# HGRN head outputs turned by VectorE in squares of 32 and put in place by their stores, instead of TensorE products with the identity

## The chip, the cores and the metric

The kernel runs on one core of one Trainium2 chip, as one program with one launch. The metric is the device time in microseconds (us) of that launch. A comparison of two versions goes by medians of several runs on the same chip.

## The reference, cut to what matters

A layer takes x, 1024 tokens of 1024 features, normalises it, projects it with `w_in` to some 5,600 columns and runs three causal mixers on them: a Mamba-2 SSD with 16 heads, an HGRN2 recurrence with 4 heads of 128, and an S5 with 32 groups. Their outputs, 2048 features in all, are multiplied with `w_out`, normalised again and added to x. Everything is float32. The change touches the HGRN part only:

```python
def hgrn2_mixer(q, f_raw, i_in, g, lb, norm_w):
    ...
    def step(state, inp):
        qc, kc, vc, lfc = inp
        cum = jnp.cumsum(lfc, axis=2)
        decay = jnp.exp(jnp.where(mask, cum[:, :, :, None, :] - cum[:, :, None, :, :], -jnp.inf))
        attn = jnp.einsum("bhlk,bhsk,bhlsk->bhls", qc, kc, decay)
        o = (jnp.einsum("bhls,bhsv->bhlv", attn, vc)
             + jnp.einsum("bhlk,bhkv->bhlv", qc * jnp.exp(cum), state))
        ...
    _, o = lax.scan(step, state0, (to_chunks(q), to_chunks(k), to_chunks(i_in), to_chunks(log_f)))
    o = o.transpose(1, 0, 3, 2, 4).reshape(bsz, seqlen, HGRN_WIDTH)
    return grouped_rms_norm(o, norm_w, HGRN_HEADS) * jax.nn.silu(g)
```

The normalisation runs over the 128 values of one head at one token. In the kernel it is done while tokens lie on the partitions (one token, one partition), since the sum then runs along a row. The product with `w_out`, much later, wants features on the partitions. So each head's normalised output, 1024 tokens by 128 values, has to be turned: eight squares of 128 by 128.

## The kernel before, in words

**Products.** TensorE computes nearly everything that is a matrix product. The large projections (`project`, `side_by_side`, `values`) and the output product split each float32 operand into a high and a low part of a rounded format (fp32r) and add three products (`mm3`); these are the rows `p<-r,v`, `p<-y,r`, `p<-s,v` and `c<-s,s` of the profile. A projection of one block of 128 columns is 48 such products of 128x512. The small products of the three mixers stay plain float32: rows with `m`, `h` or `ident` behind the arrow, which write the PSUM tiles `c` (four of them, given out in turn). Some use the whole array (128 wide), some only squares of it: the HGRN decay products are 32 wide and 64 wide, the last products of an SSD chunk 64 wide.

**An HGRN head** (`hgrn_core`, four times). Seven levels of a binary decay tree: at each level TensorE multiplies k with q' (32 small products, or 16, or 8), and VectorE multiplies k and q' by that level's decay. VectorE must wait until TensorE has read k, and TensorE's next level needs the new k, so a head is a chain of round trips between the two; projections of other columns stand between the levels on TensorE. Then k is turned by eight TensorE transposes into `kt`, seven products with `kt` give the states, VectorE chains them, and 15 products give the head's output `pss` in two PSUM tiles. ScalarE squares it, VectorE sums, a reciprocal root and a few tiny operations make the scale `ms`, and two VectorE multiplications write the normalised output to the tile `ot`. At the end, eight transposes (`T.transpose`, a product with the identity `ident`) write `ot` turned into two PSUM tiles, two ScalarE copies move these to the tile `o_`, and one store on SP's queue puts `o_` into the scratch tensor `hm_d` in DRAM, 512 bytes per piece. `out_gate` reads `hm_d` in the last part of the kernel.

**The order of the work.** It isn't that of the source. `trunk` records every instruction of the five engines, `depends` works out what each needs, and `improve` plays a list scheduler (`arrange`) forwards and backwards over them with a cost for each kind of instruction; `force` then fixes the resulting order on every engine and on the DMA queues. Each engine works strictly in that order. `BYTES` and `TRIP` are the planner's transfer rate and landing time, `KEEP` is how strongly it avoids changing TensorE's kind of product (or ScalarE's function table), `ROOMS` are margins it adds to durations and hand-offs, and `SHUFFLES` lists the planner's rounds: seed of a random shake of the ranks, its size, number of passes, and which row of `ROOMS` is in force. So an edit anywhere can move instructions everywhere.

SP issues nearly all stores and loads in its fixed order; the weight loads stand in ScalarE's queue.

Of the kernel before, what the change touches and what calls it, by code (L numbers as in the profile page):

```python
# [16 lines left out]
P = 128  # L17
# [3 lines left out]
NCH = L // P  # L21
# [155 lines left out]
    return steps + [x for *_, x in turn]  # L177


SWITCH, LOAD, BYTES, TRIP, LANES = 165.0, 1283.0, 370.0, 2000.0, 8  # L180

STEP, KEEP = 130.0, {"PE": 3000.0, "Activation": 3000.0}

ROOMS = (
    {"PE": (1.0, 200.0), "DVE": (1.06, 100.0), "Activation": (1.05, 100.0), "Pool": (1.1, 100.0)},
# [1 line left out]
    {"PE": (1.0, 300.0), "DVE": (1.06, 200.0), "Activation": (1.05, 200.0), "Pool": (1.05, 200.0)},  # L187
)

SHUFFLES = ((70, 1000.0, 4, 2), (148, 100.0, 0, 2), (165, 30.0, 1, 2), (285, 100.0, 0, 2), (331, 30.0, 0, 2), (355, 30.0, 0, 2), (376, 100.0, 0, 2), (442, 30.0, 0, 2), (529, 100.0, 0, 2), (630, 30.0, 0, 2), (726, 100.0, 0, 2))  # L190


def arrange(steps, rank, back=False):
# [92 lines left out]
def improve(steps, rank):  # L286

    plain = [(s.len, s.post) for s in steps if s.eng]
    for seed, by, passes, room in SHUFFLES:
        for s, (n, post) in zip((s for s in steps if s.eng), plain):  # L290
# [20 lines left out]
def trunk(ctx: ExitStack, tc: tile.TileContext, a: dict, out: bass.AP, dbg=None):  # L311
    nc = tc.nc
    book, bundles = [], []
    V, A, G, T, S = [Engine(e, book) for e in (nc.vector, nc.scalar, nc.gpsimd, nc.tensor, nc.sync)]
# [33 lines left out]
    def get(kind):  # L348
        return pools[kind].pop(0)

    def free(*ts_):
        for t in ts_:
            kind, t0 = home[t.tensor.name]
            pools[kind].append(t0)
# [11 lines left out]
    def ring(kind):  # L366
        t = banks[kind].pop(0)
        banks[kind].append(t)
        return t

    def slot():
        return get("m")
# [4 lines left out]
    def bank():  # L377
        return ring("c")
# [4 lines left out]
    def mul(eng, o, x, y):  # L383
        eng.tensor_tensor(out=o, in0=x, in1=y, op=ALU.mult)
# [23 lines left out]
    def mm3(o, lh, ll, rh, rl, start, stop):  # L408
        T.matmul(o, lh, rh, start=start, stop=False)
        T.matmul(o, lh, rl, start=False, stop=False)  # L410
        T.matmul(o, ll, rh, start=False, stop=stop)

    def total(o, x, h, l, eng=None):

        split(x, h, l, eng or V)
        T.matmul(o, onesr, h, start=True, stop=False)
        T.matmul(o, onesr, l, start=False, stop=True)

    def load_const(name, shape, dt=F32, src=None):
        t = cst.tile(shape, dt, tag=name, name=name)  # L420
        S.dma_start(t, a[name] if src is None else src)
        return t
# [12 lines left out]
    def c3(x, c=4):  # L435
        return x.rearrange("p (c l) -> p c l", c=c)
# [5 lines left out]
    HS = [slice(0, HALF), slice(HALF, L)]  # L442
# [33 lines left out]
    def side_by_side(ms, ps, each=lambda k: None):  # L476

        ws = [weights(a["w_in"][m]) for m in ms]
        for k in range(KD):
            each(k)  # L480
            for w, p in zip(ws, ps):
                wh, wl = [c3(t)[:, k % 4] for t in w[k // 4]]
                for n in range(2):
                    mm3(p[n], wh, wl, hh[k][:, HS[n]], hl[k][:, HS[n]], k == 0, k == KD - 1)
            if k % 4 == 3:
                for w in ws:
                    free(*w[k // 4])
# [5 lines left out]
    def begin(ms):  # L493
# [22 lines left out]
        for k in range(KD):  # L516
            h, l = get("r"), get("r")
            hf, i = k // 4, k % 4
            for t in range(2):
                if i == 0:  # L520
                    ws[t].append((get("v"), get("v")))
                if k < 2:
                    cols = (head, rest)[k]
                    split(wr[t][:, cols], *[x[:, cols] for x in ws[t][0]], V)
                elif i == 0:
                    split(wr[t][:, HS[hf]], *ws[t][hf], V)
                if t == 0:
                    for s in HS if k == 0 else [slice(0, L)]:
                        act(h[:, s], xs[k][:, s], AF.Copy, scale=prew[:, k:k + 1])
                        stt(l[:, s], xs[k][:, s], prew[:, k:k + 1], h[:, s].bitcast(F32), ALU.mult, ALU.subtract)  # L530
                wh, wl = ws[t][hf]
                for n in range(2):
                    mm3(ps[t][1][n], c3(wh)[:, i], c3(wl)[:, i], h[:, HS[n]], l[:, HS[n]], k == 0, k == KD - 1)
            if i == 3:
                for w in ws:
                    free(*w[hf])
            hh.append(h)
            hl.append(l)
            sq = acc if k == 0 else get("x")
            act(sq, xs[k], AF.Square)  # L540
            if k > 0:
                add(V, acc, acc, sq)
                free(sq)
# [35 lines left out]
    with tc.high_priority(offset=2 * PRI):  # L579
        first, rsb = begin((F0, Q0))  # L580

        ps = [[bank(), bank()], [bank(), bank()]]
        side_by_side((U0, U0 + 1), ps)
        for b in range(2):
            t = get("x")
# [12 lines left out]
    ident = load_const("ident", [P, P])  # L598
# [28 lines left out]
    def scratch(name, shape):  # L627
        return dr.tile(shape, F32, name=name)
# [3 lines left out]
    hm_d = scratch("hm_d", [NCH, P, 4, P])  # L632
# [115 lines left out]
    def hgrn_core(hd, f, k, q, v):  # L748
        qp, at, tots = slot(), slot(), slot()
# [13 lines left out]
        def product(qq, h=None, t=1):  # L763

            ps = bank()
            n = 32 if h is None else 16
            for c in range(NCH):
                for j in range(4):
                    s = slice(c * P + 32 * j, c * P + 32 * j + 32)
                    o, x = ps[32 * j:32 * j + 32, c * n:(c + 1) * n], qq[:, s]  # L770
                    if h is not None:
                        x = x.rearrange("p (n t h) -> p n t h", t=2, h=h)[:, :, t, :]
                        o = o.rearrange("p (n h) -> p n h", h=h)
                    T.matmul(o, k[:, s], x, start=True, stop=True)
            return ps[:, 0:NCH * n].rearrange("p (c l) -> p c l", c=NCH)
# [20 lines left out]
        for h in (1, 2, 4, 8, 16, 32, 64):  # L796
            n = L // (2 * h)
            tv = tot.rearrange("p (n t) -> p n t", t=2)
            if h == 2:

                A.copy(q.rearrange("p (n h t) -> p n h t", h=2, t=2)[:, :, :, 0], halves(qp, h)[:, :, 1, :])
                ps = product(q)
# [3 lines left out]
            elif h == 32:  # L806
                ps = bank()
# [5 lines left out]
                for j in range(4):  # L813
                    b, t = j // 2, j % 2
                    A.copy(at.rearrange("p (c t l) -> p c t l", t=2, l=P)[64 * b:64 * b + 32, :, t, 64 * b + 32:64 * b + 64],
                           ps[32 * j:32 * j + 32, 0:4 * 32].rearrange("p (c l) -> p c l", l=32))
            elif h == 64:

                ps = bank()
# [23 lines left out]
        for hf in range(2):  # L843
            ps = bank()
# [5 lines left out]
        for hf in range(2):  # L850
            ps = bank()
            for c in range(4):
                i = hf * 4 + c
# [4 lines left out]
            for c in range(4):  # L858
                i = hf * 4 + c
# [10 lines left out]
        ot, o_ = slot(), slot()  # L870
# [3 lines left out]
        for hf in range(2):  # L874
            ps = bank()
            pss.append(ps)
            for c in range(4):
                i = hf * 4 + c
# [14 lines left out]
        stt(ms, zs, 1.5, ys, ALU.add, ALU.mult)  # L893
        for hf in range(2):
            mul(V, c3(ot[:, HS[hf]]), c3(pss[hf]), ms[:, hf * 4:hf * 4 + 4].unsqueeze(2).to_broadcast([P, 4, P]))
        for hf in range(2):
            ps = bank()
            for c in range(4):
                i = hf * 4 + c
                T.transpose(ps[:, c * P:(c + 1) * P], ot[:, i * P:(i + 1) * P], ident)  # L900
            A.copy(o_[:, HS[hf]], ps)
        free(ot)
        if dbg is not None:
            S.dma_start(dbg["ho"][hd], o_)
        S.dma_start(hm_d[:, :, hd, :].rearrange("c p l -> p c l"), c3(o_, NCH))
        free(o_)


# [650 lines left out]
    for _ in range(2):  # L1559
        t = get("x")  # L1560
# [116 lines left out]
```

## Time and profile before

| | |
|---|---|
| median of 3 runs | 858.48 us (857.78 to 858.52) |
| profiled execution | 858.45 us |
| its span, first to last instruction | 856.7 us |
| TensorE busy (PE) | 848.2 us, 99% of the span |
| VectorE (DVE) | 563.9 us, 66% |
| ScalarE (ACT) | 399.6 us, 47% |
| GpSimd (POOL) | 249.6 us, 29% |
| granted TensorE clock | 0.999 |

The span is what the trace shows; 1.75 us of the profiled execution lie around it. In the profile every operation that a helper records stands at line 39, so groups are told apart by the names of their tiles: `c<-ident,m` is a transpose of an `m` tile into a PSUM tile `c`, `m<-c` a copy back, `hrs` the small tile of the normalisation. A plain float32 product appears as two records, a transpose or an fp32r product as one. The duration of a TensorE record contains its way through the array and overlaps the next; what an instruction takes from the engine is the distance from its start to the next start, which the timeline shows.

### The profile page before, as it was taken

The page shows a single profiled execution, that of the slowest core. Times are in us where ns is not written, and L with a number is a line of the kernel's source. Part 1 is how long each engine was busy: PE and PEld are TensorE (multiplying, and loading weights), DVE is VectorE, ACT ScalarE, POOL GpSimd, SP SyncE. Part 2 cuts the span into 40 slices and gives each one's busy share as a digit, 9 for nine tenths or more (in the row PEclk, how much of TensorE's full clock was granted, in tenths as well). Part 3 has the DMA queues.
Part 4 walks back from the last instruction along what each step waited for, and adds up shares of the span by engine and source line. Part 5 has one row for each costly group of instructions (what it writes and reads, how often), then busy time and mean ns, then how long its engine had stood idle before and what let it go on. Part 6 is the DMA issues. An engine that isn't in the chain of part 4 may idle for free.

```text
span 856.7 us, 14902 instructions
## 1 busy us (share of the span) xinstructions
PE 848.2 (99%) x5873; PEld 707.5 (83%) x5873; DVE 563.9 (66%) x1003; ACT 399.6 (47%) x637; POOL 249.6 (29%) x224
## 2 busy tenths in 40 slices
PE   8999999999999999999999999999999999999997
PEld 6888988789887888788888887788887888888886
DVE  6978399996479686785163756677646878544521
ACT  8556145455234535244237887851736833322210
POOL 0565032433143225232321234353214232111000
PEclk9999999999999999999999999999999999999999
DMA  7323012337233432448646798756957745344110
GB/s 258 112 79 120 3 51 75 101 97 217 52 95 93 122 102 63 95 117 228 181 119 219 220 269 255 240 167 205 350 153 241 239 168 197 111 136 135 62 50 25
DMA packets 92038, 124.67 MB, mean 146 GB/s; under 512 B 8448, under 2 KB 64960, under 8 KB 91968
## 3 DMA queue, kind: packets, MB, share of 16 engines
q1 hardware_dynamic: 80880, 99.40, 37.7%
q10 hardware_dynamic: 11088, 24.32, 9.7%
q8 instruction: 46, 0.75, 0.4%
q14 instruction: 24, 0.20, 0.1%
HBM read 89.52 MB, written 34.18 MB: 144 GB/s over the span
## 4 chain that ended last, share of the span: by engine, by line
PE 92%; DVE 3%; ACT 2%; DMA 1%; issue 1%; POOL 1%; SPq 0%; DVEq 0%; ACTq 0%
PE p L39 70%; PE c L39 22%; DVE m L39 2%; ACT m L39 1%; DMA m<-in_xT 1%; ACT r L39 0%; DMA w<-in_w_in 0%; DMA w<-in_w_v 0%; POOL v L39 0%; ACT L39 0%; POOL y L39 0%; ACT v L39 0%; DVE x L39 0%; DVE s5cr L39 0%; DVE h L39 0%
## 5 line engine op out<-in xcount | busy, mean ns | idle before, releaser
L39 PE MATMUL p<-r,v 128*128 128x512 f32 (+1 forms) x2208 | 542.4, 396 | 1.3 <-ACT r L39 1.0
L39 PEld LDWEIGHTS p<-r,v 128*128 128x128 f32 x2208 | 404.7, 188 | 87.5 <-issue 4.5
L39 POOL TENSOR_TENSOR v<-w,v 128x512 fp32r<-128x512 f32 x76 | 109.0, 1437 | 281.6 <-ACT v L39 225.8
L39 ACT ACTIVATE v<-w 128x512 fp32r<-128x512 f32 (+2 forms) x90 | 55.2, 619 | 171.1 <-PE p L39 153.2
L39 DVE TENSOR_TENSOR m<-m,m 128x512 f32<-128x512 f32 (+7 forms) x114 | 100.8, 905 | 29.6 <-PE c L39 12.9
L39 PE MATMUL p<-s,v 128*128 128x512 f32 (+1 forms) x384 | 87.3, 383 | 0.0
L39 PEld LDWEIGHTS p<-s,v 128*128 128x128 f32 x384 | 70.2, 188 | 14.2
L39 PEld LDWEIGHTS c<-m,m 128*32 128x32 f32 (+2 forms) x1904 | 64.4, 127 | 13.4 <-issue 6.8
L39 ACT ACT_TABLE_LOAD x51 | 65.4, 1283 | 13.7 <-DVE x L39 9.7
L39 PE MATMUL c<-m,m 128*32 128x16 f32 (+3 forms) x1904 | 69.2, 210 | 0.0
L39 PE MATMUL p<-y,r 128*128 128x272 f32 (+1 forms) x384 | 49.4, 287 | 0.1
L39 PEld LDWEIGHTS p<-y,r 128*128 128x128 f32 x384 | 47.8, 190 | 0.2
L39 DVE SCALAR_TENSOR_TENSOR x<-p,conv_w,x 128x1023 f32<-128x1023 f32 (+2 forms) x36 | 46.0, 1278 | 2.2 <-ACT x L39 1.6
L39 ACT ACTIVATE m<-m,acol 128x128 f32<-128x128 f32 x128 | 40.6, 390 | 7.0 <-DMA m<-na_d 6.6
L39 PE MATMUL c<-s,s 128*128 128x512 f32 x192 | 43.7, 389 | 0.0
L39 PEld LDWEIGHTS c<-s,s 128*128 128x128 f32 x192 | 36.0, 188 | 7.5
L39 DVE TENSOR_TENSOR h<-c,m 128x512 f32<-128x512 f32 x8 | 5.5, 689 | 46.5 <-PE c L39 46.5
L39 DVE TENSOR_TENSOR v<-x,v 128x512 fp32r<-128x512 f32 x20 | 13.8, 692 | 30.8 <-ACT v L39 30.7
L39 ACT COPY m<-c 128x512 f32<-128x512 f32 (+2 forms) x50 | 22.0, 448 | 20.9 <-PE c L39 20.3
L39 ACT ACTIVATE v<-x 128x512 fp32r<-128x512 f32 x20 | 12.3, 627 | 40.2 <-PE p L39 40.2
L39 DVE SCALAR_TENSOR_TENSOR r<-m,pre_w,r 128x1024 fp32r<-128x1024 f32 (+1 forms) x17 | 21.8, 1293 | 8.5 <-ACT r L39 8.5
L39 POOL TENSOR_TENSOR x<-x,h 128x512 f32<-128x512 f32 x10 | 14.3, 1437 | 44.7 <-DMA h<-gs_d 25.7
(205 smaller groups left out, 978.1 us busy)
## 6 DMA issues: line engine op xcount, KB each, us to landing
w<-in_w_in ACTq DMA_DIRECT2D x38, 512.0 KB, 4.1
m<-na_d SPq DMA_DIRECT2D x16, 512.0 KB, 6.6
xc_d<-x SPq DMA_DIRECT2D x12, 512.0 KB, 3.3
q<-in_w_out SPq DMA_DIRECT2D x12, 512.0 KB, 5.1
m<-tb_d SPq DMA_DIRECT2D x16, 256.0 KB, 4.4
m<-xc_d SPq DMA_DIRECT2D x8, 512.0 KB, 4.3
zc_d<-x SPq DMA_DIRECT2D x8, 512.0 KB, 4.8
ym_d<-m SPq DMA_DIRECT2D x8, 512.0 KB, 4.1
```

What stands on the lines that cost most here:

```text
L39: made = f(*args, **kw)
```

## The change

Instead of eight transposes, two PSUM tiles and two ScalarE copies per head, one VectorE instruction turns `ot` into `o_`. It turns each 32 by 32 square by itself and leaves the squares where they are. Four stores (one per 32 partitions) then write the squares to their places in `hm_d`: 32 x 8 x 4 pieces of 32 numbers, 128 bytes each. The contents of `hm_d` and its readers are as before. Beside it the planner's numbers differ: a higher transfer rate, a longer landing time, a stronger wish to keep TensorE's kind of product, and four rounds of another row of margins in place of eleven.

```diff
-SWITCH, LOAD, BYTES, TRIP, LANES = 165.0, 1283.0, 370.0, 2000.0, 8
-
-STEP, KEEP = 130.0, {"PE": 3000.0, "Activation": 3000.0}
+SWITCH, LOAD, BYTES, TRIP, LANES = 165.0, 1283.0, 410.0, 2600.0, 8
+
+STEP, KEEP = 130.0, {"PE": 5000.0, "Activation": 3000.0}
...
-SHUFFLES = ((70, 1000.0, 4, 2), (148, 100.0, 0, 2), (165, 30.0, 1, 2), (285, 100.0, 0, 2), ...
+SHUFFLES = ((47, 1000.0, 3, 1), (95, 30.0, 0, 1), (146, 100.0, 0, 1), (162, 30.0, 0, 1))
...
+    def turned(t, x, at, step, chunk, n=NCH):
+        V.transpose(out=t, in_=x)
+        for q in range(4):
+            base = at(q)
+            S.dma_start(bass.AP(base.tensor, base.offset, [[step, 32], [chunk, n], [32 * step, 4], [1, 32]]),
+                              t[32 * q:32 * q + 32].rearrange("p (i b l) -> p i b l", b=4, l=32))
...
-        for hf in range(2):
-            ps = bank()
-            for c in range(4):
-                i = hf * 4 + c
-                T.transpose(ps[:, c * P:(c + 1) * P], ot[:, i * P:(i + 1) * P], ident)
-            A.copy(o_[:, HS[hf]], ps)
+        turned(o_, ot, lambda q: hm_d[0, 0:1, hd, 32 * q:32 * q + 1], 4 * P, 4 * P * P)
         free(ot)
-        if dbg is not None:
-            S.dma_start(dbg["ho"][hd], o_)
-        S.dma_start(hm_d[:, :, hd, :].rearrange("c p l -> p c l"), c3(o_, NCH))
         free(o_)
```

Three places of the orders are shown. The first is TensorE at the end of head 0 and the start of head 1. Before, the transposes of head 0's output (`m_123` is `ot`) stand around head 1's first product (`32x16 x32`), after 30 projection products:

```order
L39 MATMUL p_136<-r_91,v_99 128x512
L39 MATMUL p_136<-r_92,v_99 128x512
L39 MATMUL p_136<-r_91,v_100 128x512
L39 MATMUL c_140<-ident,m_123 128x128 x3
L39 MATMUL c_138<-m_121,m_125 32x16 x32
L39 MATMUL c_141<-ident,m_123 128x128 x2
L39 MATMUL c_140<-ident,m_123 128x128
L39 MATMUL c_141<-ident,m_123 128x128
L39 MATMUL p_137<-r_77,v_93 128x512
L39 MATMUL c_141<-ident,m_123 128x128
```

Now head 1's first product stands two projection products behind the last output product of head 0 (`m_114,m_119` and `m_122,m_118`), and no transposes follow:

```order
L39 MATMUL c_139<-m_114,m_119 128x128
L39 MATMUL c_139<-m_122,m_118 128x128
L39 MATMUL p_136<-r_81,v_98 128x512
L39 MATMUL p_136<-r_83,v_97 128x512
L39 MATMUL c_140<-m_121,m_125 32x16 x32
L39 MATMUL p_136<-r_84,v_97 128x512
L39 MATMUL p_136<-r_83,v_98 128x512
```

Between head 1's first and second product now stand 88 projection products; before, 43 of them and five of the transposes.

The second place is TensorE between the 64-wide level of head 0 and the transposes of its k (`m_115`), where VectorE's last multiplication of k has to come in between (`m_118` is q'). Before, ten projection products stand there:

```order
L39 MATMUL c_141<-m_118,m_115 64x64 x8
L39 MATMUL p_136<-r_77,v_98 128x512
L39 MATMUL p_136<-r_79,v_97 128x512
L39 MATMUL p_136<-r_80,v_97 128x512
L39 MATMUL p_136<-r_79,v_98 128x512
L39 MATMUL p_136<-r_81,v_97 128x512
L39 MATMUL p_136<-r_82,v_97 128x512
L39 MATMUL p_136<-r_81,v_98 128x512
L39 MATMUL p_136<-r_83,v_97 128x512
L39 MATMUL p_136<-r_84,v_97 128x512
L39 MATMUL p_136<-r_83,v_98 128x512
L39 MATMUL c_138<-ident,m_115 128x128 x3
```

Now six:

```order
L39 MATMUL c_141<-m_118,m_115 64x64 x8
L39 MATMUL p_137<-r_91,v_96 128x512
L39 MATMUL p_136<-r_77,v_97 128x512
L39 MATMUL p_136<-r_78,v_97 128x512
L39 MATMUL p_136<-r_77,v_98 128x512
L39 MATMUL p_136<-r_79,v_97 128x512
L39 MATMUL p_136<-r_80,v_97 128x512
L39 MATMUL c_138<-ident,m_115 128x128 x4
```

The third place is VectorE at the end of head 0. The turning instruction stands right behind the two multiplications by the scale (`hrs`); behind it comes a level multiplication of head 1's q' (`m_115`), which head 1's third product reads, 104 projection products behind its first:

```order
L39 SCALAR_TENSOR_TENSOR hrs<-hrs 128x8 x2
L39 TENSOR_TENSOR m_123<-c_139,hrs 128x512
L39 TENSOR_TENSOR m_123<-c_138,hrs 128x512
L39 STREAM_TRANSPOSE m_116<-m_123 128x1024
L39 TENSOR_TENSOR m_115<-m_115,m_119 128x256x2
L39 TENSOR_TENSOR m_117<-pw_im,pw_re 128x32
```

Before, the same multiplications by `hrs` were followed by small S5 parameter operations. In heads 1 and 2 the turning instruction now stands just ahead of the three convolution steps of a projection (`x<-p,conv_w,x`), in head 3 inside a row of S5 table steps.

Counted over the whole program, TensorE's rows go from 4695 products to 4663. The changes from fp32r products to plain products of the full width go from 111 to 76; the uninterrupted stretches of 32-wide products stay at 28, those of 64-wide products go from 12 to 13.

More of the change, by code (lines that the diff above doesn't have):

```diff
@@ L188 @@
 )
-SHUFFLES = ((70, 1000.0, 4, 2), (148, 100.0, 0, 2), (165, 30.0, 1, 2), (285, 100.0, 0, 2), (331, 30.0, 0, 2), (355, 30.0, 0, 2), (376, 100.0, 0, 2), (442, 30.0, 0, 2), (529, 100.0, 0, 2), (630, 30.0, 0, 2), (726, 100.0, 0, 2))
+SHUFFLES = ((47, 1000.0, 3, 1), (95, 30.0, 0, 1), (146, 100.0, 0, 1), (162, 30.0, 0, 1))
 def arrange(steps, rank, back=False):
```

## The prediction

> **What bounds the kernel now.** I read the page first, then the waits of TensorE, then a table by stage, then the timelines around the heads. The page's first part, the engines of its chain of waits, and the three lines that are the whole list of TensorE's waits:
>
> ```profile
> PE 848.2 (99%) x5873; PEld 707.5 (83%) x5873; DVE 563.9 (66%) x1003; ACT 399.6 (47%) x637; POOL 249.6 (29%) x224
> PE 92%; DVE 3%; ACT 2%; DMA 1%; issue 1%; POOL 1%; SPq 0%; DVEq 0%; ACTq 0%
> PE c L39 <- DVE ones L39: 1.1, 1, 1.1
> PE p L39 <- ACT r L39: 1.0, 2, 0.5
> PE p L39 <- DVE r L39: 0.2, 1, 0.2
> ```
>
> The sum of all waits is 2.3 us, and each is one of the start-up. By stage (us, then the busy time of each engine, clock, DMA share and GB/s):
>
> ```profile
> 0.00:14.00 14.00, 11.65 (x43) 8.14 (x43) 7.16 (x13) 10.12 (x14) 0.39 (x6) 1.00 0.84 300
> 118.00:150.00 32.00, 31.95 (x351) 26.66 (x350) 30.29 (x105) 14.86 (x20) 9.84 (x16) 1.00 0.26 83
> 150.00:190.00 40.00, 40.00 (x371) 33.22 (x370) 36.42 (x86) 18.24 (x29) 16.03 (x14) 1.00 0.32 99
> 240.00:290.00 50.00, 50.00 (x604) 41.46 (x604) 41.80 (x55) 23.09 (x34) 19.43 (x18) 1.00 0.42 109
> 340.00:400.00 60.00, 60.00 (x656) 48.93 (x655) 45.24 (x78) 27.79 (x42) 17.17 (x15) 1.00 0.51 131
> 660.00:857.00 197.00, 190.60 (x890) 159.15 (x888) 107.10 (x181) 65.04 (x111) 31.92 (x25) 1.00 0.38 129
> ```
>
> The columns behind the time are TensorE, its weight loads, VectorE, ScalarE, GpSimd. From 14 us to the last product TensorE is full in every stage, at full clock. So the time is the start (2.35 us of TensorE idle in the first 14), TensorE's own work, and a tail of some 6 us in the last stage (197.00 - 190.60). Only what changes TensorE's work, or makes it wait where it never waits now, can move the end. The last 60 rows of every engine are nearly the same in both orders, so the tail stays.
>
> **What is removed.** A stretch of TensorE's timeline with known work, with the steady rate of the products from the chain of waits as first line (start, duration, work):
>
> ```profile
> 784.33 21.34 PE p L39 x94
> 161.20 3.47 PE L39 MATMUL p<-r,v 128*128 128x512 f32 x14
> 164.60 0.69 PE L39 MATMUL c<-m,m 128*64 128x64 f32 x16
> 165.22 3.47 PE L39 MATMUL p<-r,v 128*128 128x512 f32 x14
> 168.53 1.03 PE L39 MATMUL c<-ident,m 128*128 128x128 f32 x8
> 169.32 2.53 PE L39 MATMUL p<-r,v 128*128 128x512 f32 x10
> 171.68 2.17 PE L39 MATMUL c<-m,m 128*128 128x128 f32 x18
> ```
>
> An fp32r product takes 21.34 / 94 = 0.227 us. Eight transposes hold TensorE from 168.53 to 169.32, 0.79 us; the ten products behind them take 2.36 us instead of 2.27, so 0.09 more belongs to the way back, 0.88 us for eight. The ones that go are of the same form. Head 0's stand here, three, four and one, around head 1's first level product:
>
> ```profile
> 132.67 0.49 PE L39 MATMUL c<-ident,m 128*128 128x128 f32 x3
> 133.09 0.74 PE L39 MATMUL c<-m,m 128*32 128x16 f32 x64
> 133.76 0.66 PE L39 MATMUL c<-ident,m 128*128 128x128 f32 x4
> 134.17 0.48 PE L39 MATMUL p<-r,v 128*128 128x512 f32 x1
> 134.49 0.27 PE L39 MATMUL c<-ident,m 128*128 128x128 f32 x1
> 134.51 7.77 PE L39 MATMUL p<-r,v 128*128 128x512 f32 x33
> ```
>
> Start to start, 0.42 + 0.41 + 0.02 = 0.85 us: the same price within 0.03. Four heads: 4 x 0.88 = **3.5 us** of TensorE's path.
>
> ScalarE loses eight copies, and three of 51 table loads by the count of the orders:
>
> ```profile
> L39 ACT COPY m<-c 128x512 f32<-128x512 f32 x26 | 14.8, 587 | 15.2 <-PE c L39 14.8
> L39 ACT ACT_TABLE_LOAD x51 | 65.4, 1283 | 13.7 <-DVE x L39 9.7
> ```
>
> That is 8 x 0.587 + 3 x 1.283 = 8.5 us on an engine that is 47% busy and for which TensorE waits only at the start: nothing on the path.
>
> **What moves on TensorE.** The new order enters plain full-width products from fp32r products 76 times, not 111. What such a visit costs by itself shows in a shorter one:
>
> ```profile
> 203.46 0.60 PE L39 MATMUL c<-ident,m 128*128 128x128 f32 x4
> 203.81 5.40 PE L39 MATMUL p<-y,r 128*128 128x256 f32 x43
> ```
>
> Four transposes take 0.35 us, the eight above 0.79: (0.79 - 0.35) / 4 = 0.11 each, and eight at 0.11 would be 0.88. So the stretch is 0.09 us shorter at its end, which the return then takes back: the edges cost nothing, 35 fewer visits are worth nothing, and the bounds are 0 and 35 x 0.09 = 3.2 us. A change to squares of the array is dearer: in the stretch above, the 28 products around the 64-wide visit take 3.40 + 3.31 = 6.71 us instead of 6.36, so 0.35 us lie at its edges and the edge of the visit before; 0.24 to 0.35, I take **0.3 us**. There is one more such visit (13 for 12), as one SSD chunk's products stand in two halves. The 32-wide stretches stay at 28.
>
> **What is added on VectorE.** Four instructions of 128x1024. No such form is in the trace. The nearest rows, one input and the slowest that moves as much:
>
> ```profile
> L39 DVE TENSOR_SCALAR m<-m,lbm 128x1024 f32<-128x1024 f32 x4 | 4.0, 1002 | 0.4 <-ACT m L39 0.4
> L39 DVE TENSOR_SCALAR m<-m,lbm,lbt 128x1024 f32<-128x1024 f32 x4 | 5.2, 1296 | 0.0
> L39 DVE SCALAR_TENSOR_TENSOR m<-m,m 64x1016 f32<-64x1016 f32 x4 | 9.0, 2242 | 0.1
> ```
>
> So 1.0 to 2.24 us each; I take 1.3, as it reads one tensor and writes one, 5.2 us in all. What hides it: in head 0 the operation behind it is head 1's q', whose reader on TensorE stands 104 projection products behind, 104 x 0.227 = 23.6 us. In heads 1 and 2 three convolution steps stand behind it, and they hold a PSUM tile of a projection:
>
> ```profile
> L39 DVE SCALAR_TENSOR_TENSOR x<-p,conv_w,x 128x1023 f32<-128x1023 f32 x12 | 15.3, 1277 | 1.6 <-ACT x L39 1.6
> ```
>
> Three of 1.28 and the new 1.3 make 5.1 us, and there are two such tiles, the other filled by 48 products, 48 x 0.227 = 10.9 us. In head 3 it stands among table steps that a later S5 batch reads. So nothing reaches TensorE at 1.3, and at 2.24 the cover still holds (6.1 of 10.9). What is tight is VectorE as a whole from 118 to 150 us: 32.00 - 30.29 = 1.7 us free.
>
> The Trainium skill, "VectorE: DVE Perf Modes", section "The three transpose paths", gives 311 ns for a 128x128 square in bf16 on VectorE; by it, as an estimate, eight squares take 2.5 us, outside my rows. With that the slower rival below would cost 4 x 2.5 - 3.2 more than before, 865 us instead of 864. The sum stays, since the cover does. No run here shows it yet.
>
> **What is added on the queues.** Sixteen stores for four on SP's queue; each of 1024 pieces of 128 bytes:
>
> ```profile
> L39 SPq DMA_DIRECT2D hm_d<-m x4: 360/374/377, 135.9 to 394.8; - x4
> hm_d<-m SPq DMA_DIRECT2D x4, 512.0 KB, 4.3
> q1 hardware_dynamic: 80880, 99.40, 37.7%
> ```
>
> Twelve more issues are 12 x 0.374 = 4.5 us of SP over 260 us, hidden as SP mostly waits for its producers. Behind the stores on SP stand stores of convolution outputs (`xc_d`) and loads of S5 inputs, wanted tens of microseconds later. The store's own reader is the last part of the kernel, after 600 us. A packet of SP's queue takes 0.377 x 856.7 x 16 / 80880 = 64 ns, at 1229 bytes on the mean; by bytes, 128 would take 6.7 ns. So a head's 4096 packets cost each of 16 DMA engines 256 x 6.7 = 1.7 us to 256 x 64 = 16.4 us, beside shares of 0.26 to 0.51 in these stages. Scaling by bytes is the nearer end, as the mean is made by large packets. Nothing waits for them on the path.
>
> The Trainium skill, "DMA: Bandwidth & Descriptors", section "Specifications", puts line rate at 512 bytes and more, with a read-modify-write below; it speaks against 128-byte stores. By that rule the price moves up between my two bounds, and the sum changes only if the last rival comes true.
>
> **Hand-offs.** The new order has less filler at one shown place: six products, 6 x 0.227 = 1.36 us, between head 0's 64-wide level and the transposes of its k, where ten (2.27) stood. VectorE's multiplication must come in between:
>
> ```profile
> 117.54 1.29 DVE L39 TENSOR_TENSOR m<-m,m 128x512 f32<-128x512 f32 x2
> 115.52 1.29 DVE L39 TENSOR_TENSOR s5cr<-s5cr,m 128x32 f32<-128x32 f32 x1
> ```
>
> The first of those two takes some 0.65 us, so 1.36 holds it with the hand-offs, but not together with a small operation that is stretched to 1.29, as one was just before. Bounds: nothing, to the whole stretch of 1.3 us at such a place. A gain is excluded, as TensorE waits nowhere there now. I take **0.2 us** for all.
>
> **Sum.** 858.45 (profiled; span 856.7 and 1.75 around it) - 3.5 + 0.3 + 0.2 = 855.45. The median of the runs shown is 858.48, the same within 0.03, so **855.5 us**.
>
> **The rivals.** *The hand-offs eat the gain.* The new order keeps each head's small products closer together, with other margins; four heads with one wait of 0.5 us each add 2.0: 857.5. For it: the thinner filler above. Against it: 104 and 88 products where 43 stood, and no wait now in any of these places.
>
> *VectorE becomes the bound in the heads* (the slower one). The turning stands ahead of work for the next levels; if it isn't covered, TensorE waits its length in each head. At 2.24 us: 858.45 - 3.2 + 4 x 2.24 = 864.2. It decides from 3.2 / 4 = 0.8 us per head, and is slower by over 0.2% from 1.2. For it: 30.29 of 32.00 us busy. Against it: the readers behind it are 5 to 23 us away.
>
> *Small packets hold up the weight loads.* These share the DMA engines; a projection's 10.9 us of products cover a late load. It decides from 10.9 / 256 = 43 ns a packet; at 64 ns, 5.5 us a head, and four make 858.45 - 3.2 + 22 = 877; at 50 ns, 4 x 1.9 = 7.6, 863. Against it: half of the DMA time is free in these stages.
>
> *More is gained.* If the return's 0.09 us is lost at every visit, 35 fewer are worth 3.2 us more: 852.3. Against it: the shortening at the end of each visit shown above. That the products don't go is no rival: the count of the new order is 32 lower.
>
> **How the numbers follow.** The forecast gets 0.59, with a range of its own of 854.3 to 856.5; the thin hand-offs 0.22; VectorE 0.09; the packets 0.04; the larger gain 0.06. A measurement of this kernel can tell 0.2%, 1.7 us, from no change: below 856.8 is faster, above 860.2 slower. Faster: 0.59 + 0.06 + 0.05 of the hand-offs = 0.70. Same: 0.17 of the hand-offs and 0.01 of VectorE = 0.18. Slower: 0.08 + 0.04 = 0.12. The range reaches from 853.6, which leaves the larger gain out, to 858.6, which takes in the hand-offs and leaves the two slow cases: some 0.19 outside.
>
> **What would show it.** TensorE's transposes x128 instead of x160, its busy time some 3 us lower, its list of waits still only that of the start; four VectorE instructions of 1.0 to 2.24 us; stores of `hm_d` x16. It is wrong if TensorE waits for VectorE tiles `m` in the heads (hand-offs, VectorE), for weight tiles `v` after head stores (packets), or if the span falls by over 4.5 us.

## The result, and the profile after

The changed kernel takes 866.25 us (median of 6 runs, 865.61 to 868.79) beside 858.57 (857.78 to 859.42) for the kernel before: a ratio of 1.0092, interval 1.0078 to 1.0106. It is slower by 7.7 us; 855.5 was forecast, with a range of 853.6 to 858.6. The profiled execution took 865.65 us, its span 863.9.

The busy times of the engines and the engines of the chain of waits, from the page after:

```profile
PE 847.4 (98%) x5841; PEld 705.2 (82%) x5841; DVE 576.3 (67%) x1007; ACT 389.4 (45%) x626; POOL 252.5 (29%) x224
PE 85%; DMA 6%; DVE 4%; issue 2%; ACT 2%; SPq 1%; POOL 1%; ACTq 0%; DVEq 0%; POOLq 0%
```

TensorE still sets the time, with 32 instructions fewer. But it is idle for 863.9 - 847.4 = 16.5 us, where it was idle for 856.7 - 848.2 = 8.5, and its share of the chain that ended last falls from 92% to 85%, while that of DMA rises from 1% to 6%. The whole list of TensorE's waits (total us, times, longest):

```profile
PE p L39 <- DVE v L39: 2.2, 1, 2.2
PE c L39 <- ACT btt L39: 2.1, 2, 1.1
PE c L39 <- DVE ones L39: 1.1, 1, 1.1
PE c L39 <- DVE m L39: 1.0, 1, 1.0
PE p L39 <- ACT v L39: 0.7, 1, 0.7
PE p L39 <- ACT r L39: 0.6, 1, 0.6
PE p L39 <- ACT m L39: 0.6, 2, 0.3
PE p L39 <- DVE x L39: 0.6, 1, 0.6
PE c L39 <- ACT m L39: 0.6, 1, 0.6
PE p L39 <- DVE r L39: 0.2, 1, 0.2
PE c L39 <- ACT t L39: 0.2, 1, 0.2
```

That is 9.9 us, against 2.3 before. Four rows (`ones`, `v` from ScalarE, and the two of `r`, 2.6 us) are the start-up. The other 7.3 us are new, and only the 1.0 us for `m` lies in an HGRN head: it is head 0's hand-off from the 64-wide level to the transposes of k, at 117 us. All the rest lies where the edit touched nothing: the SSD copies `btt` at 526 and 534 us, an `x` of the convolution at 320, and the largest near the end, at 676.

The waits are not the whole of it. Stretches of time after, with the busy time of TensorE, its weight loads, VectorE, ScalarE and GpSimd, and then the granted clock:

```profile
677.00:680.00 3.00, 1.20 (x5) 0.79 (x5) 2.97 (x7) 2.97 (x6) 0.00 (x0) 1.00 0.33 97
680.00:683.00 3.00, 3.00 (x9) 2.32 (x8) 3.00 (x3) 2.97 (x4) 2.67 (x2) 0.54 0.89 256
```

Shortly behind the wait of 2.2 us, which ends at 678.6, the clock is granted at about half for 3.4 us (680.2 to 683.6 by the clock's own records). TensorE is busy all that time and gets half of it done, so in this execution 1.7 us are lost inside its busy time, where no list of waits shows them. Not every execution of the change has this stretch; the last section comes back to it.

The groups that the change made or thinned (busy us, mean ns); the `hm_d` stores (least, median and longest ns of an issue on SP); and SP's queue:

```profile
L39 DVE STREAM_TRANSPOSE m<-m 128x1024 f32<-128x1024 f32 x4 | 5.0, 1241 | 0.0
L39 PE MATMUL c<-ident,m 128*128 128x128 f32 x128 | 18.4, 273 | 1.0 <-DVE m L39 1.0
L39 ACT COPY m<-c 128x512 f32<-128x512 f32 x18 | 10.2, 590 | 14.5 <-PE c L39 14.4
```

```profile
L39 SPq DMA_DIRECT2D hm_d<-m x16: 303/580/1622, 133.1 to 422.1; - x16
```

```profile
q1 hardware_dynamic: 93360, 99.40, 37.9%
```

The edit did what it was to do: 128 transposes for 160, eight copies and three table loads fewer (48 for 51), four turns of 1.24 us. So the work went away as forecast, and the time came back as waits in other places. The experiments ask whether the turn, its stores or the order makes those waits.

### The profile page after: what moved, and what is told of

It is laid out like the page before. It is cut to its first block, busy times and chain, and to the rows that moved or that the text cites. A ratio compares the mean times of both kernels' runs of the same rounds, so it can differ in the third digit from the quotient of the medians.

```text
span 863.9 us, 14834 instructions
## 1 busy us (share of the span) xinstructions
PE 847.4 (98%) x5841; PEld 705.2 (82%) x5841; DVE 576.3 (67%) x1007; ACT 389.4 (45%) x626; POOL 252.5 (29%) x224
## 3 DMA queue, kind: packets, MB, share of 16 engines
q1 hardware_dynamic: 93360, 99.40, 37.9%
## 4 chain that ended last, share of the span: by engine, by line
PE 85%; DMA 6%; DVE 4%; issue 2%; ACT 2%; SPq 1%; POOL 1%; ACTq 0%; DVEq 0%; POOLq 0%
PE p L39 64%; PE c L39 20%; DVE m L39 2%; DMA zc_d<-x 1%; DMA kx<-h 1%; ACT m L39 1%; DMA pmask<-in_pmask 1%; DMA m<-in_xT 1%; DMA q<-in_w_out 1%; DVE x L39 1%; SPq L39 1%; DMA m<-kx 1%; POOL h L39 1%; DVE h L39 0%; DMA w<-in_w_in 0%
## 5 line engine op out<-in xcount | busy, mean ns | idle before, releaser
L39 PE MATMUL p<-r,v 128*128 128x512 f32 (+1 forms) x2208 | 536.3, 395 | 2.3 <-ACT v L39 0.7
L39 PEld LDWEIGHTS c<-m,m 128*32 128x32 f32 (+2 forms) x1904 | 62.4, 127 | 13.7 <-issue 6.5
L39 PE MATMUL c<-m,m 128*32 128x16 f32 (+3 forms) x1904 | 67.2, 210 | 0.6 <-ACT m L39 0.6
L39 DVE SCALAR_TENSOR_TENSOR m<-m,ssd_d,c 128x128 f32<-128x128 f32 x64 | 17.9, 342 | 14.9 <-PE c L39 14.8
L39 DVE SCALAR_TENSOR_TENSOR r<-m,pre_w,r 128x1024 fp32r<-128x1024 f32 (+1 forms) x17 | 25.4, 1513 | 3.0 <-ACT r L39 2.8
```

Of the source, the lines that this page charges most:

```text
L39: made = f(*args, **kw)
```

## The experiments

### The order of before, kept

The turn and its stores as in the change, but every instruction that both kernels have stands in the order of before, read from a table. The turn stands right behind the two multiplications that feed it, the four stores where the one stood.

```diff
-    force(tc, steps, improve(steps, [-STEP * s.ins.bass_priority if s.eng else 0.0 for s in steps]))
+    force(tc, steps, kept_order())
...
         turned(o_, ot, lambda q: hm_d[0, 0:1, hd, 32 * q:32 * q + 1], 4 * P, 4 * P * P)
+        for _ in range(2):
+            bank()
```

(The two calls of `bank` only keep the PSUM tiles given out in the same turn as before. In the change that turn is another too; it was not tried alone, but the second kernel of the next part keeps the turn of before and is slow all the same.)

> The output is turned by VectorE and stored in 128-byte pieces as in the change, but every other instruction keeps its place in the order of the kernel before: the 32 transposes and 8 copies are struck out, the turning stands behind the second multiplication by hrs, the four stores where the one stood. Theory ORDER (the loss comes from where the planner put everything else): TensorE loses 3.5 us and waits nowhere new but for at most some tenths, 855 to 856 us, 0.3% to 0.4% faster than before. Theory TURN (VectorE's 1.24 us and the small stores themselves delay TensorE): about as slow as the change or in between, 860 to 866 us, with TensorE waiting for VectorE tiles m in the heads.

Measured: 858.69 us (10 runs) beside 858.03; ratio 1.0007, interval 0.9998 to 1.0017. Each beside its own runs of before, the change loses 7.7 us and this kernel 0.7, so 7.0 of the 7.7 go with the order: the same edit in the old order is no slower that can be told. It isn't faster either, though TensorE's busy time is 845.1 us, 3.1 below before, and the time lies between what the two theories expected. Its new waits:

```profile
PE c L39 <- DVE m L39: 1.8, 2, 1.0
PE c L39 <- ACT x L39: 1.1, 1, 1.1
PE p L39 <- DVE x L39: 0.7, 1, 0.7
```

These are 3.6 us, as much as the products were worth. SP at head 2's store, with the load behind it, in this kernel and then before:

```profile
295.71 3.17 SPq L39 DMA_DIRECT2D hm_d<-m  x4
298.92 0.66 SPq L39 DMA_DIRECT2D m<-us_d  x1
```

```profile
295.96 0.38 SPq L39 DMA_DIRECT2D hm_d<-m  x1
296.38 0.59 SPq L39 DMA_DIRECT2D m<-us_d  x1
```

Four issues hold SP 3.17 us instead of 0.38, and the S5 load behind them starts 2.5 us later (298.92 for 296.38). TensorE waits 1.07 us at 301 us for the products of that load. (The list names `ACT x`; the load is argued here from the place, and shown by the four-stores kernel below.)

### The planner's numbers, old and new

Three kernels let the planner make its order anew. The first is the change with the numbers of before, the second the kernel before with the numbers of the change, the third the change with the old row of margins in its four rounds.

```diff
 the change, planned with the numbers of before
-SWITCH, LOAD, BYTES, TRIP, LANES = 165.0, 1283.0, 410.0, 2600.0, 8
+SWITCH, LOAD, BYTES, TRIP, LANES = 165.0, 1283.0, 370.0, 2000.0, 8
-STEP, KEEP = 130.0, {"PE": 5000.0, "Activation": 3000.0}
+STEP, KEEP = 130.0, {"PE": 3000.0, "Activation": 3000.0}
-SHUFFLES = ((47, 1000.0, 3, 1), (95, 30.0, 0, 1), (146, 100.0, 0, 1), (162, 30.0, 0, 1))
+SHUFFLES = ((70, 1000.0, 4, 2), (148, 100.0, 0, 2), (165, 30.0, 1, 2), (285, 100.0, 0, 2), ...
 the change, with the old row of margins
-SHUFFLES = ((47, 1000.0, 3, 1), (95, 30.0, 0, 1), (146, 100.0, 0, 1), (162, 30.0, 0, 1))
+SHUFFLES = ((47, 1000.0, 3, 2), (95, 30.0, 0, 2), (146, 100.0, 0, 2), (162, 30.0, 0, 2))
```

> The turning and the small stores as in the change, but the planner's four numbers and its list of rounds as before, so it plans anew with them. Theory ORDER says nothing of the sign of one draw: the list of rounds was made for another set of instructions, so anything from 855 to 868. If the new numbers (longer landing time, stronger wish to keep a kind of product, margins row 1) are the cause, 855 to 858; if the turning itself is, 862 to 868.

> The kernel before with its TensorE transposes, but the planner's numbers and rounds of the change. If the numbers are the cause of the loss: 858.5 + 7.7 + 3.2, some 866 to 870 us, with the same kind of waits on TensorE. If the turning is the cause: 857 to 860. By theory ORDER a draw of its own, slower than before by several us as the rounds are not those that were left without a wait: 860 to 870.

> The change with one thing different: the four planner rounds use the margins of row 2 (300 ns more for TensorE's hand-offs) as before, not row 1 (none). If the thin hand-offs of row 1 are the cause: TensorE's waits outside the start fall from some 8 us to under 3, 857 to 860 us. If they are not: 863 to 870, another draw.

Measured: 892.58 us (ratio 1.0400, interval 1.0384 to 1.0416), 868.38 (1.0120, 1.0105 to 1.0135) and 879.31 (1.0250, 1.0235 to 1.0266). The first and the third are slower than anything that was expected of them (up to 868 and up to 870). The second turns nothing and is no faster than the change, as expected if the planner's numbers make the loss. The two longest rows of the first kernel's waits, two rows of the second's, and the longest of the third's:

```profile
PE p L39 <- ACT v L39: 9.1, 3, 8.5
PE c L39 <- POOL h L39: 5.0, 1, 5.0
```

```profile
PE p L39 <- DVE v L39: 1.7, 3, 1.1
PE c L39 <- ACT t L39: 0.9, 1, 0.9
```

```profile
PE p L39 <- ACT v L39: 9.3, 3, 8.4
```

So the loss doesn't need the turn, and putting the old row of margins back doesn't mend it: with it the same rounds are 13 us worse. Every new order has new waits: with the change's own there are four such orders, and they took 7.7, 10.4, 21.3 and 34.6 us more than before. The numbers of before give a good order with the products, and a poor one with the turn. The four have one weak place in common: between 668 and 706 us, around the products `p<-s,v`, TensorE waits 2.4 us in the change, 4.3 in the second kernel (the two rows shown, 0.8 for `v` from ScalarE and 0.8 for `h`), 15.0 in the third and 13.5 in the first. The order of before waits nowhere there.

### What the old order pays for the turn and for the stores

All three keep the order of before. The first leaves the turning out altogether: no transposes, no copies, no turn, one store, so that each head's output reaches `hm_d` unturned (the two multiplications by the scale write `o_` themselves). The second keeps products and copies and adds the turn, whose result the copies overwrite. The third keeps products and copies and stores with four stores of 128-byte pieces, whose pieces go to the places of the change's squares.

```diff
 left out
-        turned(o_, ot, lambda q: hm_d[0, 0:1, hd, 32 * q:32 * q + 1], 4 * P, 4 * P * P)
+        S.dma_start(hm_d[:, :, hd, :].rearrange("c p l -> p c l"), c3(o_, NCH))
 products and the turn
+        V.transpose(out=o_, in_=ot)
         for hf in range(2):
             ps = bank()
 products and four stores
-        S.dma_start(hm_d[:, :, hd, :].rearrange("c p l -> p c l"), c3(o_, NCH))
+        for q in range(4):
+            at = hm_d[0, 0:1, hd, 32 * q:32 * q + 1]
+            S.dma_start(bass.AP(at.tensor, at.offset, [[4 * P, 32], [4 * P * P, NCH], [128 * P, 4], [1, 32]]),
+                              o_[32 * q:32 * q + 32].rearrange("p (i b l) -> p i b l", b=4, l=32))
```

> In the order of the kernel before, the 32 transposes and 8 copies are struck out and nothing takes their place: the second multiplication by hrs writes the stored tile itself, and the one old store of 512-byte pieces writes it unturned, so the heads' outputs lie untransposed in hm_d (that part of the computation is left out). It is TensorE's 3.5 us alone. Theory ADDED WORK (VectorE's 1.24 us and the longer issue of four stores made the four new waits of 3.5 us in the old order): 855 to 855.6, no new waits. Theory FILLER (without the products TensorE simply arrives early at what VectorE hasn't finished): 857 to 858.7, with waits for VectorE at 146 and 154 us of 0.5 us and more.

> The kernel before in its own order, with its products and copies, plus the four turning instructions on VectorE, whose result the copies then overwrite. It is VectorE's 4 x 1.24 us alone. Theory ADDED WORK: waits of TensorE for VectorE tiles m in head 1's levels near 146 and 154 us, 859.5 to 861. Theory FILLER: VectorE has room while the products are there, 858 to 858.8.

> The kernel before in its own order, products and copies as they were, but each head's turned tile goes out in four stores of 1024 pieces of 128 bytes; the pieces go to the places of the change's squares, so hm_d is wrongly filled. It is the stores alone. If SP's longer issue (3.17 us for four against 0.38 for one near 296 us) is what delayed the S5 load and made the wait of 1.07 us at 302 us: that wait is there again, 859 to 859.8. If the stores cost nothing by themselves: 858 to 858.6.

Measured, all beside 858.13 us: left out 855.11 (ratio 0.9961, interval 0.9946 to 0.9977); with the turn added 858.84 (1.0005, 0.9996 to 1.0014); with four stores 859.58 (1.0016, 1.0007 to 1.0025). So the products were worth 3.0 us, the forecast 3.5 lying inside the interval of 2.0 to 4.6; ADDED WORK expected this time, FILLER 857 or more. The turn by itself costs some 0.5 us or nothing (the upper end of what FILLER expected), the stores 1.4 (0.6 to 2.1), as expected if the long issue delays the load. The one new wait of each of the last two kernels:

```profile
PE c L39 <- DVE m L39: 1.0, 1, 1.0
```

```profile
PE c L39 <- DMA m<-us_d: 1.3, 1, 1.3
```

The first is at 154 us, behind head 0's turn, one of the two that ADDED WORK expected, and the second at 300 us, behind head 2's stores: the load that the four issues delay, now named. Added up, -3.0 + 0.7 + 1.4 gives -0.9, while the kernel with all three measured +0.7 (-0.2 to +1.5); the intervals of the three parts leave this difference open. The waits tell more: two of its four (0.75 us at 146, 0.69 at 197) are in neither kernel with one part added. Of the one at 197, 0.26 us stand in the kernel with the products left out, where VectorE has nothing more to do: there TensorE comes earlier. For the rest, that TensorE comes earlier and VectorE later is argued, not shown.

### Only where it costs nothing

If the price is a matter of places, heads 2 and 3 should keep the gain: they are turned in the order of before, with head 2's four stores three places later on SP, behind the `us_d` load. Heads 0 and 1 keep products and copies. A second kernel turns head 1 too, some 20 us after its output is ready, in a stretch in which VectorE idles.

```diff
+        if hd < 2:
+            (products, copies and one store as before)
+        else:
             turned(o_, ot, lambda q: hm_d[0, 0:1, hd, 32 * q:32 * q + 1], 4 * P, 4 * P * P)
 in the second kernel
-        if hd < 2:
+        if hd < 1:
```

> The old order; heads 0 and 1 keep products, copies and the one store; heads 2 and 3, where VectorE has idle stretches of some 5 us right behind, are turned by VectorE, and head 2's four stores stand three places later on SP, behind the last S5 load and the kx pair. TensorE loses 1.76 us. Theory ADDED WORK: no new wait, 856.6 to 857.0, 0.2% faster than before. Theory FILLER: 857.5 to 858.5.

> As the kernel with heads 2 and 3 turned in the order of before, and head 1 turned as well: its turn stands on VectorE behind the last m<-m,m before the idle stretch of 19 us at 206 us, its four stores on SP ahead of the loads m<-tb_d that fill the same tiles again. Head 0 keeps its products and copies. Nothing is left out. If a head is worth its 0.88 us of products wherever its turn and its stores wait for nobody, the time is 856.22 - 0.88 = 855.3 us, 0.33% under before. Rival, the stores on SP hold up the us_d and tb_d loads behind them, which TensorE needs at 224 us: a new wait there of 1 us or more, and 856.5 us or above.

Measured: 856.22 us (9 runs) beside 858.13, ratio 0.9979, interval 0.9969 to 0.9988; with three heads 856.34 (9 runs) beside 858.37, 0.9976, 0.9966 to 0.9985. Both are faster than the kernel before, by 1.9 and 2.0 us; two heads were to give 2 x 0.88 = 1.8 (856.6 to 857.0 us). The whole list of waits with two heads turned, and the one row that the list with three has beside these:

```profile
PE c L39 <- DVE ones L39: 1.1, 1, 1.1
PE p L39 <- ACT r L39: 0.7, 1, 0.7
PE p L39 <- DVE r L39: 0.2, 1, 0.2
```

```profile
PE p L39 <- DVE x L39: 0.3, 1, 0.3
```

The first is that of the start-up alone: the gain stays where the turn and the stores stand in front of nobody. The third head's 0.88 us isn't shown: 855.3 us was expected, its profiled span is 0.7 us shorter, 0.3 go to a wait at 196 us, and the two ratios can't be told apart. The wait at 224 us which the rival expected didn't come.

### The change's own order, with single faults taken out

Here the change's order is the table, and single instructions are moved. First the product `v<-x,v`, for which TensorE waits longest. TensorE and VectorE of the change at that place (start, duration, work):

```profile
678.61 0.49 PE L39 MATMUL p<-s,v 128*128 128x512 f32 x1 [2.23 <-DVE v L39]
```

```profile
672.82 1.37 DVE L39 TENSOR_TENSOR x<-x,h 128x512 f32<-128x512 f32 x2 [1.14 <-DMA h<-zc_d]
...
676.53 1.41 DVE L39 TENSOR_TENSOR h<-h 128x256 f32<-128x256 f32 x4 [1.02 <-ACT h L39]
677.87 0.68 DVE L39 TENSOR_TENSOR v<-x,v 128x512 fp32r<-128x512 f32 x1
```

```diff
 VectorE, first kernel
+v<-x,v
 x<-x,h x2
 h<-h,h x2
 h<-h x4
-v<-x,v
 second kernel, besides
 VectorE: head 0's last m<-m,m of k four small operations earlier (not six, as expected below)
 ScalarE: btt<-c ahead of three m<-m,acol (526 us)
 ScalarE: btt<-c ahead of three m<-m,acol and one m<-m (534 us)
```

> The change with every instruction in the change's own order, but for one: VectorE's product v<-x,v, which ran at 677.87 us behind two additions x<-x,h, two scalar-tensor-tensor operations and four h<-h, stands ahead of the two additions (672.82 us). Nothing is left out. If the order alone makes the loss, TensorE's 2.2-us wait at 676.0 us is gone (under 0.3 us left there), and the time is 866.25 - 2.2 = 864.0 us; if the half granted clock of 680.2 to 683.6 us comes from that wait, another 3.4 / 2 = 1.7 us goes and the time is 862.3 us. Rival, the turn itself or its stores cost the 8 us and waits only show it: the wait moves to the next place and the time stays within 0.5 us of 866.2.

> As the kernel with one instruction moved, and three more: head 0's last product m<-m,m ahead of the six small operations before it on VectorE (the 0.97-us wait at 117.2 us), and two copies btt<-c on ScalarE ahead of three activations with acol (527.56 us, the wait of 1.08) and ahead of three activations with acol and one of 1024 elements (535.21 us, the wait of 1.05). Nothing is left out. If these waits are faults of the order that stand by themselves, each goes, and the time is 3.1 us under that of the kernel with one moved: 859.2 us if that one is at 862.3, 860.9 if it is at 864.0. Rival, what is gained at one place is lost at the next hand-off: under 1 us below the kernel with one moved.

Measured: 865.65 us (ratio 1.0088, interval 1.0074 to 1.0102), 0.6 under the change, which the intervals don't tell from nothing, where 2.2 or more were expected; with all four moved 863.22 (1.0059, 1.0043 to 1.0074). At the longest wait of the first, and in the list of the second, stands

```profile
679.36 0.38 PE L39 MATMUL c<-t,onesr 128*128 128x256 f32 x1 [2.36 <-ACT t L39]
```

```profile
PE c L39 <- ACT t L39: 2.5, 1, 2.5
PE c L39 <- ACT btt L39: 0.9, 1, 0.9
```

So the first expectation failed, and what its rival said of the wait came true: with `v` in time, TensorE waits as long for the next thing, the sums of the normalisation over `t`. That the turn or its stores stand behind it, as the rival had it, isn't shown by this, and the kernel without a turn that waits at the same place speaks against it. The three other moves gave 2.4 of the 3.1 us: head 0's wait shrank from 1.0 to 0.4, and one of the two for `btt` is gone. The other copy then stood behind a store in ScalarE's queue.

What makes the chain up to `t` late? TensorE from the products ahead of the block `c<-s,s` on, before, and then in the change:

```profile
594.10 12.31 PE L39 MATMUL p<-r,v 128*128 128x512 f32 x53
606.24 43.68 PE L39 MATMUL c<-s,s 128*128 128x512 f32 x192
649.76 5.60 PE L39 MATMUL p<-r,v 128*128 128x512 f32 x24
655.20 1.02 PE L39 MATMUL c<-h,ones 128*128 128x512 f32 x2
655.66 6.04 PE L39 MATMUL p<-r,v 128*128 128x512 f32 x24
661.54 1.02 PE L39 MATMUL c<-h,ones 128*128 128x512 f32 x2
```

```profile
598.40 14.57 PE L39 MATMUL p<-r,v 128*128 128x512 f32 x63
612.81 43.68 PE L39 MATMUL c<-s,s 128*128 128x512 f32 x192
656.33 5.37 PE L39 MATMUL p<-r,v 128*128 128x512 f32 x23
661.54 1.02 PE L39 MATMUL c<-h,ones 128*128 128x512 f32 x2
662.00 2.17 PE L39 MATMUL p<-r,v 128*128 128x512 f32 x7
```

Between the first sum `c<-h,ones` and the product that waits stood 24 + 48 products before, and 7 + 48 and three `p<-s,v` stand there now: 14 fewer, 3.2 us of cover at 0.227 us each. Ten of them are spent ahead of the block, 63 for 53. So the last kernel moves the block 16 products up, repairs the copies and head 0's product, and puts `v<-x,v` back.

```diff
 TensorE
 p<-r,v x47
-p<-r,v x16
 c<-s,s x192
+p<-r,v x16
 p<-r,v x23
 ScalarE: btt<-c also ahead of the store ys_d<-m (526 us)
```

> The change with its own order, but for four places. On TensorE the block of 192 products c<-s,s (612.81 to 656.3 us) stands 16 products p<-r,v earlier, so that 39 and not 23 of these lie between it and the first c<-h,ones, as they do before (24 there, 24 more ahead of the second). On ScalarE one copy btt<-c stands ahead of the store ys_d<-m at 526.29 us that waits, and one ahead of three activations with acol and one of 1024 elements (535.21 us). On VectorE head 0's last product m<-m,m of the first kind stands ahead of four small operations. v<-x,v is back where the change has it. Nothing is left out. Theory, the wait of 2.2 us at 676.0 us comes from TensorE's order alone, which has spent products ahead of the block that hid the chain behind it: that wait goes with its half clock (2.2 + 1.7 us), the copies' and head 0's waits go too (3.1 us), and the time is 866.25 - 7.0 = 859.3 us, between 858.3 and 860.3. Rival, the chain behind the block is late by other engines (the loads, ScalarE's activations): the wait of over 2 us stays, and the time is 862.5 us or above.

Measured: 865.38 us (ratio 1.0085, interval 1.0068 to 1.0102), neither the 859.3 of the theory nor a proof of the rival. Its two longest waits, and the stretch behind each, with the granted clock in the third column from the end:

```profile
PE c L39 <- ACT s L39: 2.6, 1, 2.6
PE p L39 <- DVE v L39: 1.7, 1, 1.7
```

```profile
608.00:611.00 3.00, 2.94 (x7) 2.36 (x8) 2.46 (x3) 2.01 (x4) 0.00 (x0) 0.51 1.02 393
679.00:682.00 3.00, 2.92 (x8) 2.44 (x9) 3.00 (x4) 2.39 (x4) 2.09 (x1) 0.53 0.83 216
```

Both waits for `btt` are gone, and head 0's is 0.4 again. But the block now waits 2.6 us for its first operand, which ScalarE makes behind a weight split and a copy that wait for TensorE, and behind a load, in an order made for the later time. And the expectation had an error: the products went between the block and the first sum, not behind that sum, so the chain to `t` had no more cover than in the change, and a wait of 1.7 us stayed. With each goes, in this execution, a stretch at half clock. What follows: the small waits are single faults, each gone once an instruction or two moves; the long one went away neither with one move on VectorE nor with one on TensorE. That the orders of the engines there fit each other only together is argued. Which move, if any, frees the place at 676 us stays open.

## Why the prediction was wrong, point by point

**The bound** was right: TensorE from start to end. Busy 847.4 and idle 16.5 make up the span after, too.

**What is removed** was right: 3.5 us forecast, 3.0 measured with an interval of 2.0 to 4.6, and 1.9 for two heads. ScalarE's work fell by 399.6 - 389.4 = 10.2 us for the forecast 8.5 and was worth nothing, as said.

**The turn** was sized right, 1.24 us for 1.3. In the change no wait lies behind it: behind the turns of heads 1 and 2 VectorE idles 2.0 and 6.2 us. In the old order it cost one of 1.0 us at head 0, where VectorE had 1.7 us free in 32; the cover named in the prediction held for the new order only. The Trainium skill, "VectorE: DVE Perf Modes", section "The three transpose paths", led to an estimate of 2.5 us from its bf16 figure; the traces show 1.24 for the same eight squares in float32, and the measurement decides. The rival "VectorE becomes the bound" fell.

**The stores** were half right. The packets were harmless: by the trace's own records one of 128 bytes takes 13 ns in the median (27 for 512 bytes), twice the nearer bound of 6.7 and far under the 43 at which they would decide. With 12,480 more of them the queue's share went from 37.7% to 37.9%, and the only waits for weight tiles `v` are those of the start-up (the `v` of 2.2 us is made of `x`). The section "Specifications" of the Trainium skill's "DMA: Bandwidth & Descriptors", which puts line rate at 512 bytes and more, agrees so far as a byte of the small packets takes twice as long; it changed nothing of the time here. The issue was mis-sized: 0.374 us each in the prediction, a median of 0.58 measured, and a mean of 0.79 (3.17 / 4) for the four of head 2 in the old order. That the issues are "hidden as SP mostly waits for its producers" was false at this place, where they cost 1.07 to 1.3 us.

**The hand-offs** are the step that failed: "A gain is excluded, as TensorE waits nowhere there now. I take 0.2 us for all." The place that it named did wait, 0.97 us, inside its bounds and for the reason that it gave: VectorE's last multiplication of k starts at 117.86 us, behind a small operation of 128x32 that took 1.18. But the term looked only at the heads, and it took the freedom from waits for a property of the kernel, when it was one of a particular order. The new order differs nearly everywhere, and it waits 7.3 us behind the start-up. By terms, in the profiled execution: with 3.5 us of products gone the span would be 853.2, and it is 863.9, 10.7 more. Waits make 7.6 of these (9.9 for 2.3) and the half clock 1.7; 1.4 are left, for which the sum had 0.5 and whose origin no run shows. The rival "the hand-offs eat the gain" had the mechanism, with 2.0 us in the heads as its price; it should have been priced over the whole span.

The prediction could have had this. The diff changed the planner's rounds and the order moved almost everywhere, and the list of waits before, empty behind the start-up, shows that another order could only add waits.

## What to carry to other kernels

When an edit makes a planner or a fixed order start afresh, price the new order apart from the edit: keep the old order with the edit in it, and compare. In a kernel whose bounding engine never waits, a new order can only add waits (all four here did), and here the gain was kept where the added instructions stand in front of nobody, head by head. On a queue in strict order, count what each added issue delays behind it, with the longest issue of that form and not that of the form it replaces.

## What was unexpected of the hardware

Past the start-up, in the profiled executions, the granted clock stood at about half for 3.4 us around the end of each wait of TensorE of 1.7 to 2.6 us (five of them in the change and the three kernels made from its order, and two, of 2.0 and 2.1 us, in the kernel planned with the numbers of before), and at none of those up to 1.3 us. Around that kernel's waits of 5.0 and 8.5 us it stood at half for 20.5 us. TensorE does half its work in such a stretch, so one of 3.4 us takes 1.7 us of it and lowers the mean clock of a run by 0.002.

What this costs in the end isn't settled. Of the six runs of the change one has a mean clock of 0.999, which leaves no room for the stretch, and it took 865.61 us; the others, at 0.994 to 0.997, took 865.65 to 868.79. With four instructions moved, two runs at 0.999 took 863.17 and 863.27, two at 0.996 took 863.11 and 863.72. So not every execution has the stretch behind the same wait, and those without it aren't 1.7 us shorter. In the start-up, where waits of 0.4 to 1.0 us follow each other closely, such a stretch stands in some profiled executions (the kernel with one instruction moved has it, the change doesn't), which can blur comparisons of single executions. The Trainium skill, "TensorE: Matmul & The Clock Gate", section "What's actually happening", tells of windows of about 3.4 us and of an idle window of that length before the clock halves; the length of the slow stretch agrees, while here less idle time was enough.

An issue of 1024 pieces on SP's queue isn't one price: in the change 0.58 us in the median and up to 1.62 with pieces of 128 bytes, where pieces of 512 bytes took 0.37 before. It hangs on the place too: head 2's four took 3.17 us together in the old order, and 6.10 three places later on SP in the kernel with two heads turned. And turning 128x1024 float32 values in squares of 32 takes VectorE 1.24 us, within 3% of the 1.28 us of a convolution step on as many values.
